# Group C's pooling behind group D's attention, with its two halves handled together

## The chip, the core and the metric

The kernel runs on one core of a Trainium2 chip. The metric is the device time of one execution in microseconds. Three runs of the kernel before gave 1563.94, 1564.75 and 1565.75 us; their median, 1564.75 us, is what a change is held against.

## The reference

Two layers of a transformer block over 512 latent and 256 context tokens, 1024 features each, all in 32-bit numbers. Each layer modulates and normalises its input, projects it, and gives the columns to four groups of 256 channels: A (windowed attention), B (gated position mixing), C (pooling), D (attention over a 2-D neighbourhood). Their outputs are joined, projected, gated and added; a feed-forward part follows. The last layer computes group C for the latent tokens alone. Group C is this:

```
for gi, w in enumerate((2, 4, 8, 16)):       # 64 channels each
    lo, hi = clip(t - w // 2, 0, n), clip(t - w // 2 + w, 0, n)
    pooled = (cs[:, hi] - cs[:, lo]) / (hi - lo) - y     # centred mean less the token
    outs.append(pooled @ w_pool[gi])
out_c = concatenate(outs) * scale
```

## The kernel before

Tokens lie along the free axis, 128 channels on the partitions. A layer begins with projections for group C (two tiles of 128 channels, c = 0 and 1) and for D's values, straight from the scaled input; c = 0 lands in the two pj banks of PSUM, c = 1 in the two sc banks, D's values in po, pt, tq and md. While they run, the normalised input h is made (L311 on POOL, L313 on DVE, L314 on ACT, L315 on DVE). L266 copies the shift out of PSUM.

Then come, in program order: the pooling of both c (c_pool), D's values, the query and key projections of D's first pair of heads (d_proj; in the last layer d_ctx before it makes the context keys of both pairs), the end of C (c_fin), the attention of pair 0 (d_group), the projections and the attention of pair 1, and then groups A and B. A projected tile goes through post_qk: ACT squares it (L479), DVE sums (L481), takes an inverse root in ten small steps (L100 to L109), multiplies (L484, which frees the pj or sc bank, and L486), PE transposes it into the one tq bank (L510), ACT and DVE write the query (L525, L526) and the key (L531 to L533) out of it. In the attention DVE takes the scores out of sc (L628, L630), ACT the exponential (L359), PE transposes (L337) and multiplies (L349), ACT copies the result to the mix tile (L354).

c_pool multiplies the PSUM tile by r (L788), ACT adds the shift (L789), POOL clears the margins (L784) and builds the sums over windows by repeated additions (L792 and L793 for c = 0, L795 to L798 for c = 1). Channels 0 to 63 end in one buffer and 64 to 127, with the wider window, in another, so DVE handles the halves one after the other: the edges (L806), then the scaling less the token (L807). L92 and L93 split the result into a high and a low part. c_fin multiplies by the pooling weights (wph) and ACT scales the result into the mix tile (L819).

What sets the order: the source fixes no order between engines. A planner simulates the whole program and gives each engine its queue; among instructions that are ready, the earlier one in the program goes first. On the chip each engine then works its queue in that order. Buffers have tags, each with so many buffers (BUFS and BANKS). Within a tag the planner gives them out in the order of the tiles' first writes in the program: a later tile gets none before the earlier ones have theirs. The st tag has 8 buffers. The eight scaled inputs fill it first; then come three tiles for each c (b1, b2, ph), then the keys and queries of D's pairs (the key's low half is cleared on POOL, L556, which needs nothing but the buffer), then those of A. The bias tag has 2; one of them holds wph until c_fin(1) is done, the others hold the bias tiles of the heads, which POOL builds (L612) from a table that SP loads (L606).

Of the kernel before, what the change touches and what calls it, by code (L numbers as in the profile page):

```python
# [8 lines left out]
F32 = mybir.dt.float32  # L9
F32R = mybir.dt.float32r  # L10
I32 = mybir.dt.int32
AF = mybir.ActivationFunctionType
OP = mybir.AluOpType
# [5 lines left out]
SEQ = 512  # L19
CTX = 256  # L20
NT = SEQ + CTX
# [7 lines left out]
BIG = 1e30  # L29
W = 24 + NT  # L30
BUFS = {"h": 8, "x": 8, "st": 8, "w": 6, "raw": 3, "mraw": 2, "T": 3, "pts": 3, "bias": 2, "row": 3, "post": 4,
        "br": 1}
BANKS = {"pj": 2, "sc": 2, "tq": 1, "pt": 1, "po": 1, "md": 1}
MAGIC = float(0x5F3759DF)
GELU_C = 0.7978845608028654
# [4 lines left out]
def hybrid_block(ctx: ExitStack, tc, t, out):  # L40
    nc = tc.nc
    V, S, G, T = nc.vector, nc.scalar, nc.gpsimd, nc.tensor
# [3 lines left out]
    small = ctx.enter_context(tc.tile_pool(name="small", bufs=4))  # L46
# [3 lines left out]
    def tile(tag, shape, dtype=F32):  # L50
        return sb.tile(shape, dtype, tag=tag, name=tag, bufs=BUFS[tag])
# [212 lines left out]
    def shift_of(cuts, pss):  # L264
        sh = small.tile([128, 2], F32, tag="sh", name="sh")
        V.tensor_copy(sh, pss[1][:, cuts[1]:cuts[1] + 2])  # L266
        return sh
# [117 lines left out]
    for l in range(DEPTH):  # L385
        last = l == DEPTH - 1
        segs = segs_lat if last else segs_all
# [11 lines left out]
        if l == 0:  # L399
# [3 lines left out]
            for what, k in START.split():  # L403
# [15 lines left out]
                if what + str(k) == "s5":  # L419
                    r = norm_spread(rr, segs_all, ("md", "md"))  # L420
            first = ws
            mods.append(new_mod(1))
        else:
            r = norm_spread(norm_scale(sq, segs_all), segs_all, ("tq", "tq"))
            first = [feat_units(*x) for x in first]
        fcuts = [cuts_lat if last else cuts_all] * 2 + [cuts_all]
        pss = [[psum(x) for x in y] for y in (("pj", "pj"), ("sc", "sc"), ("po", "pt"))]
# [13 lines left out]
        if l == 0:  # L441
# [3 lines left out]
            edge = const_tile("edge", [128, 2, 3, 8], t["edge"])  # L445
# [16 lines left out]
        V.memset(wpool, 0.0)  # L462
        for j in range(2):
            nc.sync.dma_start(wpool[64 * j:64 * j + 64, :, 64 * j:64 * j + 64], t["wpool"][l, j])
        wph = tile("bias", [128, 2, 256], F32R)
        split_to(wph[:, 0], wph[:, 1], wpool.rearrange("p a b -> p (a b)"))

        def lhs_nat(k, z, i):
# [100 lines left out]
        def d_proj(p, K=None):  # L569
            w = group_units("win_d", p)  # L570
            bs = (0, 2) if K else tiles
            K = K or d_keys()
            Q = tile("st", [128, 2, NT], F32R)
            for bi, b in enumerate(bs):
                ps = tok_proj(w, b, 0, 256, [["pj", "sc", "pj"], ["pj", "pj", "pj"]][p][bi])
                post_qk(ps, b, 2, 2, gd, 2, False, [Q], K, True)
            return Q, K
# [22 lines left out]
        mix = [None] * KT  # L600
# [176 lines left out]

        pos = {0: 8, 1: 16 + SEQ}

        def c_pool(c, pss):  # L780
            b1, b2 = tile("st", [128, 2, W]), tile("st", [128, 2, W])
            y, sA = b1[:, 0], b1[:, 1]
            sB, res = b2[:, 0], b2[:, 1]
            G.memset(y, 0.0)  # L784
            sh = shift_of(fcuts[0], pss)
            for (_, _, s0, s1, v, o), ps in zip(fcuts[0][0], pss):
                yv = y[:, pos[v] + s0 - SEQ * v:pos[v] + s1 - SEQ * v]
                V.tensor_mul(yv, ps[:, o:o + s1 - s0], r[:, s0:s1])  # L788
                S.activation(yv, yv, AF.Identity, bias=sh[:, v:v + 1])  # L789

            if c == 0:
                G.tensor_add(res[:, 1:W], y[:, 0:W - 1], y[:, 1:W])  # L792
                G.tensor_add(sA[64:128, 2:W - 1], res[64:128, 1:W - 2], res[64:128, 3:W])  # L793
            else:
                G.tensor_add(sA[:, 1:W], y[:, 0:W - 1], y[:, 1:W])  # L795
                G.tensor_add(sB[:, 2:W - 1], sA[:, 1:W - 2], sA[:, 3:W])
                G.tensor_add(res[:, 4:W - 3], sB[:, 2:W - 5], sB[:, 6:W - 1])
                G.tensor_add(sA[64:128, 8:W - 7], res[64:128, 4:W - 11], res[64:128, 12:W - 3])  # L798
            ph = tile("st", [128, 2, NT], F32R)
            for s0, s1, v in segs:  # L800
                n = s1 - s0
                o = pos[v]
                for q0, q1, src in ((0, 64, res), (64, 128, sA)):

                    for e, o1 in ((0, o), (1, o + n - 8)):
                        V.tensor_mul(src[q0:q1, o1:o1 + 8], src[q0:q1, o1:o1 + 8], edge[q0:q1, c, e])  # L806
                    V.scalar_tensor_tensor(sB[q0:q1, o:o + n], src[q0:q1, o:o + n], edge[q0:q1, c, 2, 0:1],  # L807
                                           y[q0:q1, o:o + n], op0=OP.mult, op1=OP.subtract)
                split_to(ph[:, 0, s0:s1], ph[:, 1, s0:s1], sB[:, o:o + n])
            return ph  # L810

        def c_fin(c, ph):
            mix[4 + c] = tile("x", [128, NT])
            for s0, s1, v in segs:
                n = s1 - s0
                ps = psum(["sc", "po", "sc", "tq"][2 * c + v])
                mm3(ps[:, :n], wph[:, 0, 128 * c:128 * c + 128], wph[:, 1, 128 * c:128 * c + 128],
                    ph[:, 0, s0:s1], ph[:, 1, s0:s1], True, True)
                S.activation(mix[4 + c][:, s0:s1], ps[:, :n], AF.Copy, scale=csc[:, c:c + 1])  # L819


        def d_group(p, Q, K, Vt):
            mix[6 + p] = tile("x", [128, NT])
            d_pair(p, Q, K, Vt)
            if not last:
                for i in (4, 5):
                    ctx_pair(i, Q, K[0], K[1],
                             [[Vt[:, x, 64 * hh:64 * hh + 64] for hh in range(2)] for x in (4, 5)], None, mix[6 + p])
# [9 lines left out]
                             nsink[:, p:p + 3:2], mix[p])  # L838

        if last:  # L840
            ph = [c_pool(c, pss[c]) for c in range(2)]
            v0 = d_values(pss[2], "row")
            v1 = d_values(pss[3], "mraw")
            kc = d_ctx()
            q0 = d_proj(0, kc[0])
            c_fin(0, ph[0])
            c_fin(1, ph[1])
            alt[:] = ["pt", "md"]
            d_group(0, *q0, v0)
            q1 = d_proj(1, kc[1])  # L850
            d_group(1, *q1, v1)
            ga = a_proj()
            a_group(0, *ga)
            gb = b_proj()
            a_group(1, *ga)
            b_fin(*gb)
        else:
            ph = [c_pool(c, pss[c]) for c in range(2)]
            v0 = d_values(pss[2], "row")
            v1 = d_values(pss[3], "mraw")  # L860
            q0 = d_proj(0)
            c_fin(0, ph[0])
            c_fin(1, ph[1])
            alt[:] = ["pt"]
            d_group(0, *q0, v0)
            q1 = d_proj(1)
            mod_unit(4, mods[l])
            mod_gain(mods[l], 1)
            d_group(1, *q1, v1)
            ga = a_proj()  # L870
            mod_unit(2, mods[l])
            a_group(0, *ga)
            gb = b_proj()
            b_fin(*gb)
            mod_unit(3, mods[l])
            alt[:] = ["pt", "md"]
            a_group(1, *ga)
# [26 lines left out]
        for mt in range(KT):  # L904
            w = wsplit(t["wout"][l, mt])
            outs = proj_out(w, KT, mh, ORDER, [[["pj", "pj", "tq", "md", "sc", "sc", "pt", "po"], ["pj", "pj", "tq", "md", "sc", "sc", "pt", "po"]][l][(mt * len(segs) + i) % 8] for i in range(len(segs))])
            x = xs[mt]
# [180 lines left out]
```

## Time and profile before

| | us |
|---|---|
| median of three runs | 1564.75 |
| the profiled execution | 1565.54 |
| its span, first to last instruction | 1563.8 |
| PE busy in it | 1518.4 |
| DVE busy | 963.7 |
| ACT busy | 618.1 |
| POOL busy | 122.2 |

How to read it: PE is the engine of matmuls, DVE, ACT and POOL work on vectors, SP issues DMAs. A matmul's end is modelled, and matmuls overlap, so a PE that is shown busy is not PE at its peak. Layer 0 has its projections for C and D up to some 80 us, then the attention up to some 310 us; in layer 1 the same stretches are 940 to 964 and 1035 to 1150 us. The rest is the output projection and the feed-forward part, where PE stands still hardly at all.

### The profile page before, as it was taken

To read this page: it belongs to the slowest core of one execution; us is meant where nothing else is said; L and a number is where in the kernel's file an instruction comes from. 1 tells how busy PE (TensorE), PEld (TensorE's weight loads), DVE (VectorE), ACT (ScalarE), POOL (GpSimd) and SP (SyncE) were. 2 spreads that over 40 slices of the span, in tenths; PEclk is the share of its full clock that TensorE was granted. 3 is DMA by queue.
4 is the path that set the end of the run, shared out by engine and by line. 5 is a ranking of instruction groups with operands and counts; after the bars stand their busy time and mean duration, and the time that the engine had idled before them with its cause. 6 is when DMAs were issued, how large, how long until landed. Compare 5 with 4: busy or idle time off the path is not lost.

```text
span 1563.8 us, 26196 instructions
## 1 busy us (share of the span) xinstructions
PE 1518.4 (97%) x10098; PEld 1336.1 (85%) x10098; DVE 963.7 (62%) x2335; ACT 618.1 (40%) x1276; POOL 122.2 (8%) x107
## 2 busy tenths in 40 slices
PE   7889999999999999999999998899999999999999
PEld 4668888788888888888888887788889998998997
DVE  4797876686485624833384467789856543454453
ACT  5546655643322112221222354457654332332331
POOL 2431000000000000000000005632000000000000
PEclk9899999999999999999999999999999999999999
DMA  8433133342243313622272231111223333223323
GB/s 309 122 115 116 48 110 129 122 139 75 88 142 113 117 62 115 222 59 64 93 248 59 78 113 55 58 55 47 81 82 102 95 84 105 90 87 102 95 82 100
DMA packets 79325, 163.39 MB, mean 104 GB/s; under 512 B 12001, under 2 KB 17761, under 8 KB 79201
## 3 DMA queue, kind: packets, MB, share of 16 engines
q1 hardware_dynamic: 79200, 161.73, 32.8%
q8 instruction: 79, 1.29, 0.3%
q14 instruction: 46, 0.37, 0.1%
HBM read 157.50 MB, written 4.19 MB: 103 GB/s over the span
## 4 chain that ended last, share of the span: by engine, by line
PE 89%; DVE 5%; ACT 1%; issue 0%; DVEq 0%; ACTq 0%
PE pj L65 9%; PE pj L66 9%; PE pj L67 9%; PE sc L66 6%; PE sc L65 6%; PE sc L67 6%; PE tq L65 3%; PE po L349 3%; PE tq L66 3%; PE tq L67 3%; PE po L65 3%; PE po L66 3%; PE po L67 3%; PE pt L66 2%; PE pt L67 2%; PE pt L65 2%
## 5 line engine op out<-in xcount | busy, mean ns | idle before, releaser
L82 ACT ACTIVATE w<-raw 128x512 fp32r<-128x512 f32 x368 | 227.5, 621 | 640.1 <-PE sc L67 159.5
L83 DVE TENSOR_TENSOR w<-raw,w 128x512 fp32r<-128x512 f32 x336 | 227.3, 679 | 244.7 <-ACT w L82 244.2
L65 PE MATMUL pj<-w,h 128*128 128x256 f32 x480 | 141.5, 295 | 12.8 <-DVE post L484 6.7
L66 PE MATMUL pj<-w,h 128*128 128x256 f32 x480 | 140.0, 292 | 2.9 <-DVE w L83 2.9
L67 PE MATMUL pj<-w,h 128*128 128x256 f32 x480 | 139.4, 291 | 0.0
L65 PE MATMUL pj<-st,w 128*128 128x258 f32 (+2 forms) x384 | 120.6, 314 | 2.5 <-ACT st L253 2.3
L66 PE MATMUL pj<-st,w 128*128 128x258 f32 (+2 forms) x384 | 120.4, 314 | 0.7 <-DVE st L254 0.7
L66 PE MATMUL sc<-st,w 128*128 128x258 f32 (+2 forms) x384 | 120.0, 313 | 0.0
L65 PE MATMUL sc<-st,w 128*128 128x258 f32 (+2 forms) x384 | 119.9, 312 | 0.0
L67 PE MATMUL pj<-st,w 128*128 128x258 f32 (+2 forms) x384 | 119.8, 313 | 0.0
L67 PE MATMUL sc<-st,w 128*128 128x258 f32 (+2 forms) x384 | 119.2, 311 | 0.0
L65 PEld LDWEIGHTS pj<-w,h 128*128 128x128 f32 x480 | 94.4, 197 | 21.1 <-issue 9.3
L83 POOL TENSOR_TENSOR w<-raw,w 128x512 fp32r<-128x512 f32 x32 | 44.2, 1398 | 742.2 <-ACT w L82 721.7
L66 PEld LDWEIGHTS pj<-w,h 128*128 128x128 f32 x480 | 94.7, 197 | 4.4 <-DVE w L83 3.1
L67 PEld LDWEIGHTS pj<-w,h 128*128 128x128 f32 x480 | 94.3, 197 | 1.3 <-issue 1.2
L65 PEld LDWEIGHTS pj<-st,w 128*128 128x128 f32 x384 | 73.1, 191 | 9.5 <-ACT st L253 3.5
L66 PEld LDWEIGHTS pj<-st,w 128*128 128x128 f32 x384 | 72.8, 190 | 5.7 <-DVE st L254 0.9
L67 PEld LDWEIGHTS pj<-st,w 128*128 128x128 f32 x384 | 72.7, 190 | 5.7 <-issue 1.7
L65 PEld LDWEIGHTS sc<-st,w 128*128 128x128 f32 x384 | 73.2, 191 | 4.6
L66 PEld LDWEIGHTS sc<-st,w 128*128 128x128 f32 x384 | 72.8, 189 | 4.4
L67 PEld LDWEIGHTS sc<-st,w 128*128 128x128 f32 x384 | 72.4, 189 | 4.2
L65 PE MATMUL po<-st,w 128*128 128x512 f32 (+1 forms) x192 | 66.5, 346 | 0.0
(304 smaller groups left out, 4125.8 us busy)
## 6 DMA issues: line engine op xcount, KB each, us to landing
mraw<-in_wmod SPq DMA_DIRECT2D x80, 512.0 KB, 3.7
raw<-in_wg SPq DMA_DIRECT2D x88, 256.0 KB, 2.6
raw<-in_wu SPq DMA_DIRECT2D x88, 256.0 KB, 2.6
raw<-in_wd SPq DMA_DIRECT2D x64, 256.0 KB, 2.7
h<-in_wslab SPq DMA_DIRECT2D x16, 512.0 KB, 7.8
raw<-in_wout SPq DMA_DIRECT2D x32, 256.0 KB, 2.6
x<-in_xt SPq DMA_DIRECT2D x16, 384.0 KB, 5.8
raw<-in_wd SPq DMA_DIRECT2D x32, 192.0 KB, 2.4
```

Source lines behind the costliest of these rows:

```text
L65: T.matmul(ps, ah, bh, start=start, stop=False)
L66: T.matmul(ps, ah, bl, start=False, stop=False)
L67: T.matmul(ps, al, bh, start=False, stop=stop)
L82: S.activation(w[:, 0, :n], raw, AF.Copy)
L83: eng.tensor_sub(w[:, 1, :n], raw, w[:, 0, :n].bitcast(F32))
L349: T.matmul(o[64 * hh:64 * hh + 64, :128], vs[hh][lo:hi], pts[i, hh], start=i == 0, stop=i == n - 1)
```

## The change

c_pool is parted. c_take stays where c_pool was: it takes a tile of c out of PSUM with the multiplication by r, into the mix tile of c itself, and copies the shift to a small buffer of its own. The rest of c_pool moves: c_pool(0) and c_fin(0) stand behind the attention of D's pair 0, c_pool(1) and c_fin(1) behind that of pair 1. In it, ACT brings the shift in on the way from the mix tile to the padded row y; the rows end at n, which is 792 elements in layer 0 as before and 528 in the last layer; ACT copies channels 64 to 127 of the sums into the buffer of the others, and the edges, the scaling and the subtraction then run once on 128 partitions. wph gets a buffer with a tag of its own.

```diff
-        wph = tile("bias", [128, 2, 256], F32R)
+        wph = tile("wph", [128, 2, 256], F32R)
...
-        def c_pool(c, pss):
+        def c_take(c, pss):
+
+            mix[4 + c] = tile("x", [128, NT])
+            for (_, _, s0, s1, v, o), ps in zip(fcuts[0][0], pss):
+                V.tensor_mul(mix[4 + c][:, s0:s1], ps[:, o:o + s1 - s0], r[:, s0:s1])
+            sh = small.tile([128, 2], F32, tag="csh", name="csh", bufs=2)
+            V.tensor_copy(sh, pss[1][:, fcuts[0][1]:fcuts[0][1] + 2])
+            return sh
+
+        def c_pool(c, sh):
             b1, b2 = tile("st", [128, 2, W]), tile("st", [128, 2, W])
             y, sA = b1[:, 0], b1[:, 1]
             sB, res = b2[:, 0], b2[:, 1]
-            G.memset(y, 0.0)
-            sh = shift_of(fcuts[0], pss)
-            for (_, _, s0, s1, v, o), ps in zip(fcuts[0][0], pss):
-                yv = y[:, pos[v] + s0 - SEQ * v:pos[v] + s1 - SEQ * v]
-                V.tensor_mul(yv, ps[:, o:o + s1 - s0], r[:, s0:s1])
-                S.activation(yv, yv, AF.Identity, bias=sh[:, v:v + 1])
+            n = pos[segs[-1][2]] + segs[-1][1] - segs[-1][0] + 8
+            up = slice(64, 128)
+            G.memset(y[:, :n], 0.0)
+            for s0, s1, v in segs:
+                S.activation(y[:, pos[v]:pos[v] + s1 - s0], mix[4 + c][:, s0:s1], AF.Identity, bias=sh[:, v:v + 1])
...
-                G.tensor_add(sA[64:128, 2:W - 1], res[64:128, 1:W - 2], res[64:128, 3:W])
+                G.tensor_add(sA[up, 2:n - 1], res[up, 1:n - 2], res[up, 3:n])
+                S.activation(res[up, 2:n - 1], sA[up, 2:n - 1], AF.Copy)
...
-                G.tensor_add(sA[64:128, 8:W - 7], res[64:128, 4:W - 11], res[64:128, 12:W - 3])
+                G.tensor_add(sA[up, 8:n - 7], res[up, 4:n - 11], res[up, 12:n - 3])
+                S.activation(res[up, 8:n - 7], sA[up, 8:n - 7], AF.Copy)
...
-                for q0, q1, src in ((0, 64, res), (64, 128, sA)):
-
-                    for e, o1 in ((0, o), (1, o + n - 8)):
-                        V.tensor_mul(src[q0:q1, o1:o1 + 8], src[q0:q1, o1:o1 + 8], edge[q0:q1, c, e])
-                    V.scalar_tensor_tensor(sB[q0:q1, o:o + n], src[q0:q1, o:o + n], edge[q0:q1, c, 2, 0:1],
-                                           y[q0:q1, o:o + n], op0=OP.mult, op1=OP.subtract)
+
+                for e, o1 in ((0, o), (1, o + n - 8)):
+                    V.tensor_mul(res[:, o1:o1 + 8], res[:, o1:o1 + 8], edge[:, c, e])
+                V.scalar_tensor_tensor(sB[:, o:o + n], res[:, o:o + n], edge[:, c, 2, 0:1],
+                                       y[:, o:o + n], op0=OP.mult, op1=OP.subtract)
...
-            mix[4 + c] = tile("x", [128, NT])
...
-            ph = [c_pool(c, pss[c]) for c in range(2)]
+            csh = [c_take(c, pss[c]) for c in range(2)]
...
-            c_fin(0, ph[0])
-            c_fin(1, ph[1])
             alt[:] = ["pt"]
             d_group(0, *q0, v0)
+            c_fin(0, c_pool(0, csh[0]))
             q1 = d_proj(1)
...
             d_group(1, *q1, v1)
+            c_fin(1, c_pool(1, csh[1]))
             ga = a_proj()
```

The calls at the end are those of layer 0; in the last layer c_fin and c_pool move in the same way.

## Rows read from the trace of the kernel before

**Rows 1.** Of the profile's page: busy time, share and instructions of each engine
```profile
PE 1518.4 (97%) x10098; PEld 1336.1 (85%) x10098; DVE 963.7 (62%) x2335; ACT 618.1 (40%) x1276; POOL 122.2 (8%) x107
```

**Rows 2.** Stretches, as from:to and length, then each engine's busy time, clock, DMA
```profile
80.00:90.00 10.00, 8.01 (x54) 8.02 (x55) 9.31 (x25) 3.74 (x8) 1.47 (x2) 0.83 0.26 79
...
110.00:120.00 10.00, 8.02 (x46) 5.12 (x47) 8.93 (x33) 4.21 (x11) 0.00 (x0) 0.83 0.59 208
126.00:166.00 40.00, 40.00 (x335) 35.44 (x334) 32.25 (x129) 27.97 (x72) 7.84 (x11) 1.00 0.32 106
...
970.00:980.00 10.00, 7.11 (x47) 7.14 (x48) 8.23 (x21) 3.98 (x9) 3.00 (x2) 0.68 0.00 0
...
1000.00:1010.00 10.00, 6.45 (x41) 6.43 (x41) 9.04 (x31) 2.03 (x5) 3.57 (x5) 0.83 0.19 56
...
1035.00:1080.00 45.00, 45.00 (x388) 40.38 (x387) 43.00 (x165) 35.06 (x93) 15.33 (x14) 1.00 0.17 50
```

**Rows 3.** PE's waits from 76 to 122 us: total, times, longest
```profile
PE tq L510 <- DVE st L533: 3.2, 1, 3.2
PE pj L66 <- DVE w L83: 2.9, 1, 2.9
```

**Rows 4.** PE's waits from 958 to 1032 us
```profile
PE pj L65 <- DVE post L484: 6.7, 3, 3.5
PE pj L65 <- DVE st L788: 6.1, 1, 6.1
PE tq L510 <- DVE st L533: 3.5, 1, 3.5
```

**Rows 5.** DVE's groups by shape, 60 to 125, then 965 to 1010 us
```profile
L806 DVE TENSOR_TENSOR st<-st,edge 64x8 f32<-64x8 f32 x16 | 3.7, 292 | 0.1
...
L807 DVE SCALAR_TENSOR_TENSOR st<-st,edge 64x512 f32<-64x512 f32 x4 | 3.0, 747 | 0.1
...
L807 DVE SCALAR_TENSOR_TENSOR st<-st,edge 64x256 f32<-64x256 f32 x4 | 1.9, 478 | 0.0
...
L93 DVE TENSOR_TENSOR st<-st 128x512 fp32r<-128x512 f32 x2 | 1.4, 682 | 0.0
...
L806 DVE TENSOR_TENSOR st<-st,edge 64x8 f32<-64x8 f32 x8 | 3.4, 460 | 0.5 <-POOL st L792 0.4
...
L807 DVE SCALAR_TENSOR_TENSOR st<-st,edge 64x512 f32<-64x512 f32 x4 | 3.0, 748 | 0.2
```

**Rows 6.** DVE in order of time: start, length, line, operation, shape, count
```profile
77.35 3.65 DVE L315 SCALAR_TENSOR_TENSOR h<-x,mod,h 128x512 fp32r<-128x512 f32 x2
...
91.03 0.17 DVE L104 SCALAR_TENSOR_TENSOR ry<-rz,ry 128x8 f32<-128x8 f32 x1
91.22 1.38 DVE L105 TENSOR_TENSOR rz<-ry 128x8 f32<-128x8 f32 x1
...
95.89 0.69 DVE L484 TENSOR_TENSOR post<-pj,ry 128x512 f32<-128x512 f32 x1
96.61 1.37 DVE L486 TENSOR_TENSOR post<-post,d_q_gain 128x256 f32<-128x256 f32 x1
```

**Rows 7.** POOL in order of time, 60 to 130 us
```profile
91.07 1.50 POOL L795 TENSOR_TENSOR st<-st 128x791 f32<-128x791 f32 x1 [9.54 <-DVE rz L103]
...
95.85 1.85 POOL L798 TENSOR_TENSOR st<-st 64x777 f32<-64x777 f32 x1
...
103.54 3.10 POOL L556 MEMSET st<- 64x768 f32 x4
128.87 1.23 POOL L612 TENSOR_TENSOR bias<-dmask,br 128x256 f32<-128x256 f32 x1 [22.24 <-PE sc L368]
```

**Rows 8.** ACT in order of time, around 1006 and 1060 us
```profile
1005.72 0.63 ACT L92 ACTIVATE st<-st 128x512 fp32r<-128x512 f32 x1 [6.54 <-DVE st L807]
...
1057.14 0.28 ACT L354 ACTIVATE x<-po 128x128 f32<-128x128 f32 x1
...
1062.21 0.36 ACT L531 ACTIVATE st<-tq 64x256 fp32r<-64x256 f32 x1
```

More of the change, by code (lines that the diff above doesn't have):

```diff
@@ L31 @@
 BUFS = {"h": 8, "x": 8, "st": 8, "w": 6, "raw": 3, "mraw": 2, "T": 3, "pts": 3, "bias": 2, "row": 3, "post": 4,
-        "br": 1}
+        "br": 1, "wph": 1}
 BANKS = {"pj": 2, "sc": 2, "tq": 1, "pt": 1, "po": 1, "md": 1}
@@ L783, in c_pool @@
             sB, res = b2[:, 0], b2[:, 1]
-            G.memset(y, 0.0)
-            sh = shift_of(fcuts[0], pss)
-            for (_, _, s0, s1, v, o), ps in zip(fcuts[0][0], pss):
-                yv = y[:, pos[v] + s0 - SEQ * v:pos[v] + s1 - SEQ * v]
-                V.tensor_mul(yv, ps[:, o:o + s1 - s0], r[:, s0:s1])
-                S.activation(yv, yv, AF.Identity, bias=sh[:, v:v + 1])
+            n = pos[segs[-1][2]] + segs[-1][1] - segs[-1][0] + 8
[3 more added lines that the diff above has]
+                S.activation(y[:, pos[v]:pos[v] + s1 - s0], mix[4 + c][:, s0:s1], AF.Identity, bias=sh[:, v:v + 1])
             if c == 0:
-                G.tensor_add(res[:, 1:W], y[:, 0:W - 1], y[:, 1:W])
-                G.tensor_add(sA[64:128, 2:W - 1], res[64:128, 1:W - 2], res[64:128, 3:W])
-            else:
-                G.tensor_add(sA[:, 1:W], y[:, 0:W - 1], y[:, 1:W])
-                G.tensor_add(sB[:, 2:W - 1], sA[:, 1:W - 2], sA[:, 3:W])
-                G.tensor_add(res[:, 4:W - 3], sB[:, 2:W - 5], sB[:, 6:W - 1])
-                G.tensor_add(sA[64:128, 8:W - 7], res[64:128, 4:W - 11], res[64:128, 12:W - 3])
+                G.tensor_add(res[:, 1:n], y[:, 0:n - 1], y[:, 1:n])
+                G.tensor_add(sA[up, 2:n - 1], res[up, 1:n - 2], res[up, 3:n])
+                S.activation(res[up, 2:n - 1], sA[up, 2:n - 1], AF.Copy)
+            else:
+                G.tensor_add(sA[:, 1:n], y[:, 0:n - 1], y[:, 1:n])
+                G.tensor_add(sB[:, 2:n - 1], sA[:, 1:n - 2], sA[:, 3:n])
+                G.tensor_add(res[:, 4:n - 3], sB[:, 2:n - 5], sB[:, 6:n - 1])
+                G.tensor_add(sA[up, 8:n - 7], res[up, 4:n - 11], res[up, 12:n - 3])
+                S.activation(res[up, 8:n - 7], sA[up, 8:n - 7], AF.Copy)
             ph = tile("st", [128, 2, NT], F32R)
@@ L857, in hybrid_block @@
         else:
-            ph = [c_pool(c, pss[c]) for c in range(2)]
+            csh = [c_take(c, pss[c]) for c in range(2)]
             v0 = d_values(pss[2], "row")
@@ L861, in hybrid_block @@
             q0 = d_proj(0)
-            c_fin(0, ph[0])
-            c_fin(1, ph[1])
             alt[:] = ["pt"]
             d_group(0, *q0, v0)
+            c_fin(0, c_pool(0, csh[0]))
             q1 = d_proj(1)
@@ L869, in hybrid_block @@
             d_group(1, *q1, v1)
+            c_fin(1, c_pool(1, csh[1]))
             ga = a_proj()
```

## The prediction

> **What bounds the kernel now.** I read the engines' busy times first: PE is busy 97% of the span, so 45 us is all that it ever stands still [rows 1], and only a change that shortens PE's stops can pay. The stretches of ten us come next: they show where those stops lie. Apart from the start (out of reach of this change), they stand in two places, behind the first projections of each layer, where group C's pooling is done: 76 to 122 us in layer 0 and 958 to 1032 us in layer 1. There DVE is busy 8.2 to 9.3 us of ten while PE is not full, and the granted clock, once PE has stood still for 3 us and more, falls to 0.83 or 0.68 of 2.4 GHz over the slice: for a part of it, it is at its lower level of 1.2 [rows 2 to 4]. Third, PE's own waits in the two windows: in layer 0 it waits 3.2 us for L533 (DVE's last step of a query/key tile, which frees the tq bank) and 2.9 us for L83 (a weight split on DVE) [rows 3]; in layer 1, 6.7 us for L484, 6.1 us for L788 (pooling's own eviction of its PSUM bank) and 3.5 us for L533 [rows 4]. All of them are on DVE. In the attention behind it PE shows full: 40.00 of 40 and 45.00 of 45 us, with DVE at 32.25 of 40 in layer 0, but at 43.00 of 45 in layer 1 [rows 2]. So the question is what DVE is spared before the attention, and what it can't take inside it.
>
> **The change, part by part.**
> *Halves together.* L806 and L807 run once on 128 partitions instead of twice on 64. An instruction's time here goes by its elements per partition, so half of the instructions go: in layer 0 half of 3.7 + 3.0 + 1.9 us = 4.3 us, in layer 1 half of 3.4 + 3.0 = 3.2 us [rows 5]. For it ACT copies the upper half: four copies, of 789 (layer 0) and 525 elements. The nearest row is ACT's split of 512 elements at 0.63 us [rows 8]; by size 0.97 and 0.65 us, 3.2 us in all. ACT has 28 of 40 and 35 of 45 us busy there [rows 2], so I take zero, and 3.2 if they end on a chain that PE waits for.
> *Shorter rows in layer 1.* With n = 528 instead of 792, POOL's steps there shrink by a third.
> *c_take.* The multiplications by r stay, at the same place in the order, but write into an x buffer (free once the first h is made), so the second one no longer waits for c = 0 to be pooled. About 0.68 + 0.41 us of DVE (the size of the split row [rows 5] and its smaller form) comes forward in layer 0. PE's 6.1 us for L788 I leave: the multiplication still stands behind all of L313 and L315.
> *wph in its own buffer.* Today the second bias tile of pair 0 waits until c_fin(1) has given its buffer back: POOL stands 22.24 us in front of L612 in layer 0 [rows 7]. It can now run before the window. Only queued POOL work gains; nothing on PE's path, zero, and at most one L612 (1.23 us) either way.
> *Pooling moved.* Two orders hold it back. It stands behind d_group in the program, and the planner hands out st buffers in program order: POOL's clearing of the key tiles, which needs only a buffer, stands behind the whole pooling, at 103.54 us [rows 7]. The same rule now puts the pooling behind the key and query tiles of pair 0, so it can't creep forward into idle engines. It issues no DMA. c_fin's 12 and 6 matmuls move with it at the same PE time; their sc bank now comes between the scores of pair 0 and pair 1, where the second sc bank covers it: zero, up to 1.4 us a call.
>
> What leaves the early window in layer 0: three kinds of cost. DVE's own steps are the 8.6 us named above and 2.2 us of splits. POOL's six additions (1.50 to 1.85 us each, 9.7 us in all) hold DVE up: L105, a step on 8 elements, takes 1.38 us beside L795, where the like step L104 ahead of it takes 0.17 [rows 6, 7]; there are three of that kind, and with the 0.95 us of L486 and the 2.3 us lost in the pair of L315 at 77.35 us (3.65 us, where two steps of their size would take some 1.4) this is 6.9 us, 0.7 us of DVE for each us of POOL. And ACT, in order, stands 6.54 us in front of a split of the pooling in layer 1 while the key tile's L531, which frees tq, is queued behind it [rows 8].
>
> An instruction with one operand in PSUM didn't wait: L484 took 0.69 us beside L798, and L486 behind it, all in SBUF, 1.37 us [rows 6, 7]. The Trainium skill, in "SBUF — State Buffer", section "Who interferes with whom", says the same as a rule: a DVE instruction with two SBUF inputs contends with GpSimd's reads, one with at most one does not; by it, much of the attention's DVE work (L628, L630 and L533 read PSUM) would be untouched by the moved additions, and the lock terms below would be about half.
>
> *Layer 0, gained.* The 3.2 us behind L533 go with the queue ahead of it. Of the 2.9 us behind L83, the L315 pair gives back 2.3 and c_take's second multiplication takes 1.1: 1.2 us gone. Two slices at 0.83 are 3.4 us each at half speed, 1.7 us lost each [rows 2]; I count one. 3.2 + 1.2 + 1.7 = 6.1 us, between 3 and 9.5 (all of both stalls and both slices).
> *Layer 0, given back.* The attention gets 4.3 + 2.2 us of DVE steps and 0.7 x 9.7 = 6.8 us of waiting, 13.3 us. DVE has 7.75 us idle in 126 to 166 us [rows 2], and half of the load (c = 1) falls later still: between 0 and 5.5 us, nearest to 0; I take 1.5.
> *Layer 1, gained.* Behind L484 and L533 lie 10.2 us. What stands in the way there are 8.3 us of pooling on DVE, ACT's 6.54 us, and POOL's pooling; the weight splits on POOL stay and hold DVE up as before. I take two thirds, 6.8 us, and one of two slices at 0.83, 1.7: 8.5 us, between 3 and 13.6.
> *Layer 1, given back.* 3.2 us of steps, 1.4 of splits, 0.7 x 6.5 = 4.5 us of waiting: 9.1 us, where DVE has 2.0 us idle in 45 [rows 2]. Between 0 and 7.1; c = 0 has to be over before pair 1's query tile gets its buffer, so half lies earlier. 3.5, and 1.25 for group A's key tile, which now waits for the last st buffer of c = 1 (between 0 and rival B): 4.75 us.
> Sum: -6.1 + 1.5 - 8.5 + 4.75 = -8.35 us. The profiled execution took 1565.54 us (span 1563.8), 0.8 us over the median of 1564.75: 1557.2 on its scale, **1556.5 us** on the median's.
>
> **The rivals.**
> *A, the cost only moves.* DVE is the limit inside the attention too, and the page's full PE hides it: matmul times overlap, and PEld shows 40.38 of 45 us [rows 2]. Then all that is moved comes back: 5.5 + 7.1 + 1.25 and ACT's 3.2 on the chain, 17 against 14.6 gained: +2.4, about 1567 us. For it: 43.00 of 45 us in layer 1. Against: layer 0's idle DVE, and that 7.5 us are really gone. The Trainium skill, "Trainium Kernel Development and Optimization", section "Performance Expectations", calls matmul busy time a bad metric and LDWEIGHTS busy a good one, which would make this rival likelier.
> *B, slower: group A starves behind the pooling of c = 1.* Its last st buffers need pair 0's tiles back, and group A's key tile comes after them. Today the first key write (L531 at 1062.21) follows pair 0's last output (L354 at 1057.14) by 5.1 us [rows 8]. Afterwards three additions, a copy, the edges, one L807 and a split stand between: in layer 1 3.3 + 0.65 + 0.6 + 0.75 + 0.63 = 5.9 us, in layer 0 4.9 + 0.97 + 1.2 + 1.2 + 0.63 = 8.9 us. Behind a DVE that is 96% busy I put twice that: 11.8 and 17.8, later than today by 6.7 and 12.7. If PE has nothing else then, 19.4 us are lost, and with 3.5 + 1.5 of the give-back against 14.6 gained: +9.8, 1575 us. It decides from some 10 us between the last output of pair 0 and the first key write. Against it: PE has the modulation's matmuls in layer 0, and pj is projected one tile ahead.
> *C, the pooling stays early* because idle engines draw it forward; only the halving counts, 7.5 us of DVE, half on the path: 1561 us. Against it: the order of the buffers.
> *D, nothing is given back* and all stalls but L788's go: 9.5 + 13.6 = 23.1 us, 1542 us.
>
> **How the numbers follow.** Forecast 0.51 (own range 1549 to 1561.5), A 0.20, B 0.15, C 0.06, D 0.08. From 1545 to 1569 all but D and most of B is held, some 0.8. About 3.1 us, 0.2%, is what a measurement here can tell from no change. Faster: the forecast, D, half of C: 0.62. Same: most of A, the rest of C: 0.21. Slower: B and a little of A: 0.17.
>
> **What would show it.** Right: no POOL addition between the first projections and the first scores of either layer; L104 to L109 at some 0.17 us in layer 0; PE's waits for L533 gone from both windows, L788's 6 us still there; slices at 1.00 around 110 and 1000 us. Wrong on the give-back: PE idle, or fewer matmuls per ten us, between the pairs' attentions, with DVE at 100%. B: more than 10 us from pair 0's last L354 to group A's first L531, with PE idle in it. C: additions still beside L105.

## The result, and the profile after

The changed kernel takes 1556.64 us (median of 4 runs, 1555.05 to 1557.38) against 1564.36 us of the kernel before on the same chip: 7.7 us less by the medians. The ratio on record is 0.9945, 95% interval 0.9933 to 0.9957, which is 8.6 us of 1564.75 (6.7 to 10.5); the text goes by these ratios. The forecast was 1556.5. The number came out; half of its sum did not, as the experiments show.

The page of the changed kernel, profiled at 1556.92 us (span 1555.1), busy time of each engine:

```profile
PE 1514.8 (97%) x10098; PEld 1332.3 (86%) x10098; DVE 957.6 (62%) x2317; ACT 620.8 (40%) x1278; POOL 113.6 (7%) x107
```

PE has as many matmuls as before and is busy 3.6 us less [rows 1]: PE's own time has changed too, not only its stops.

The stretches, with the columns of [rows 2]:

```profile
80.00:90.00 10.00, 10.00 (x81) 9.03 (x80) 6.18 (x17) 3.87 (x7) 0.00 (x0) 1.00 0.40 133
110.00:120.00 10.00, 10.00 (x76) 7.89 (x74) 9.27 (x32) 5.51 (x12) 0.76 (x1) 1.00 0.31 105
...
970.00:980.00 10.00, 10.00 (x80) 10.00 (x80) 3.86 (x13) 4.92 (x9) 4.65 (x4) 0.93 0.21 64
1000.00:1010.00 10.00, 5.13 (x31) 4.95 (x31) 9.47 (x21) 5.92 (x12) 7.09 (x6) 0.78 0.24 79
1035.00:1080.00 45.00, 42.67 (x353) 36.56 (x352) 42.28 (x146) 32.59 (x85) 16.96 (x17) 1.00 0.18 58
```

PE's waits from 76 to 122 us, then from 950 to 1032 us (total, times, longest):

```profile
PE pj L65 <- DVE post L484: 0.6, 1, 0.6
PE pj L65 <- DVE x L784: 0.5, 1, 0.5
```

```profile
PE pj L65 <- DVE x L784: 7.2, 1, 7.2
PE pj L65 <- ACT st L532: 4.9, 1, 4.9
PE tq L510 <- DVE st L533: 0.6, 1, 0.6
```

The window of layer 0 is clear: the 6.1 us of [rows 3] are 1.1, and both slices that stood at 0.83 [rows 2] are at 1.00, with 81 and 76 matmuls for 54 and 46. In layer 1 the multiplication that empties C's bank (now L784) holds PE as long as L788 did [rows 4]; of the 10.2 us behind L484 and L533, 5.5 are left. The 4.9 us put down to L532 end on L484, which runs at 1005.80 us. In the attention of layer 1 PE has 353 matmuls in 45 us where it had 388, partly since it comes to them earlier.

How far PE has come by 120 and by 220 us, before and then after (the count behind PE's busy time is its matmuls):

```profile
0.00:120.00 120.00, 96.78 (x635) 74.09 (x636) 84.54 (x210) 61.05 (x122) 42.53 (x34) 0.93 0.54 182
...
0.00:220.00 220.00, 196.78 (x1451) 158.62 (x1452) 166.57 (x517) 125.04 (x288) 53.35 (x47) 0.96 0.43 143
```

```profile
0.00:120.00 120.00, 101.58 (x698) 79.40 (x698) 79.86 (x203) 60.85 (x121) 33.04 (x33) 0.94 0.54 188
...
0.00:220.00 220.00, 200.10 (x1484) 161.28 (x1484) 162.02 (x497) 124.34 (x286) 48.44 (x47) 0.97 0.43 146
```

At 120 us the changed kernel leads by 63 matmuls, some 8 us at 81 in ten us; at 220 us by 33.

The same instructions in both traces (us, start in the profiled execution):

| | before | after | difference |
|---|---|---|---|
| layer 0: first score of group D (L628) | 127.2 | 128.0 | +0.8 |
| its last | 200.0 | 194.5 | -5.5 |
| first of group A (L708) | 215.4 | 225.1 | +9.7 |
| its last | 301.4 | 298.5 | -2.9 |
| first FFN norm (L290) | 378.1 | 375.3 | -2.8 |
| end of the FFN of layer 0 (L290) | 941.9 | 936.5 | -5.3 |
| layer 1: first score of group D (L628) | 1036.0 | 1021.4 | -14.6 |
| its last | 1079.8 | 1072.9 | -6.9 |
| last of group A | 1143.8 | 1136.5 | -7.3 |
| FFN norm of layer 1 | 1189.4 | 1182.1 | -7.3 |
| end | 1560.8 | 1552.1 | -8.6 |

Of 8.6 us, 2.8 lie in the mixing of layer 0, 2.0 in that of layer 1, and 2.5 and 1.4 in the two FFNs, where the change touches nothing and PE stands full in both kernels. A first score can come later with PE further on: at D's first score in layer 0 PE has 763 matmuls behind it instead of 694, because projections that follow the score in the old order now run ahead of it.

### The profile page after: what moved, and what is told of

The parts are those of the page before. It is cut to its first block, busy times and chain, and to the rows that moved or that the text cites. A ratio compares the mean times of both kernels' runs of the same rounds, so it can differ in the third digit from the quotient of the medians.

```text
span 1555.1 us, 26167 instructions
## 1 busy us (share of the span) xinstructions
PE 1514.8 (97%) x10098; PEld 1332.3 (86%) x10098; DVE 957.6 (62%) x2317; ACT 620.8 (40%) x1278; POOL 113.6 (7%) x107
## 4 chain that ended last, share of the span: by engine, by line
PE 88%; DVE 6%; DMA 3%; ACT 1%; issue 1%; SPq 0%; POOL 0%; ACTq 0%; POOLq 0%
PE pj L65 9%; PE pj L66 9%; PE pj L67 9%; PE sc L65 6%; PE sc L66 6%; PE sc L67 6%; PE tq L65 3%; PE tq L66 3%; PE po L66 3%; PE po L65 3%; PE tq L67 3%; PE po L67 3%; PE po L349 3%; PE pt L66 2%; PE pt L65 2%; PE pt L67 2%
## 5 line engine op out<-in xcount | busy, mean ns | idle before, releaser
L83 DVE TENSOR_TENSOR w<-raw,w 128x512 fp32r<-128x512 f32 x336 | 226.2, 676 | 241.2 <-ACT w L82 240.5
L65 PE MATMUL pj<-st,w 128*128 128x258 f32 (+2 forms) x384 | 120.2, 314 | 1.4 <-ACT st L253 1.2
L65 PEld LDWEIGHTS pj<-w,h 128*128 128x128 f32 x480 | 93.3, 194 | 20.4 <-issue 10.4
L83 POOL TENSOR_TENSOR w<-raw,w 128x512 fp32r<-128x512 f32 x32 | 42.6, 1342 | 747.5 <-ACT w L82 723.0
L66 PEld LDWEIGHTS pj<-w,h 128*128 128x128 f32 x480 | 93.4, 195 | 1.8 <-issue 0.9
L67 PEld LDWEIGHTS pj<-w,h 128*128 128x128 f32 x480 | 93.2, 194 | 0.4 <-issue 0.3
```

Source lines behind the costliest of these rows:

```text
L65: T.matmul(ps, ah, bh, start=start, stop=False)
L66: T.matmul(ps, ah, bl, start=False, stop=False)
L67: T.matmul(ps, al, bh, start=False, stop=stop)
L83: eng.tensor_sub(w[:, 1, :n], raw, w[:, 0, :n].bitcast(F32))
```

## The experiments

Each run was compared with the kernel before on the same chip. The table has them all: the ratio with its interval, what it is in us of 1564.75, what of that lies in the FFNs' matmuls, and the rest. The FFN part is worked out from the starts of successive matmuls with a scaled x tile (st) in the trace: in layer 0 the mean step is 233.94 ns before and 232.38 after at 512 columns, 120.37 and 119.48 at 258; times 1056 of each that is 1.65 + 0.94 = 2.6 us; in layer 1, worked out alike, 1.4 us. Single executions of one kernel lie up to 5 us apart, so the verdicts go by the ratio and the traces only tell where. "The rest" is the ratio's microseconds less the FFN part; its uncertainty is that of the ratio, 1.4 to 2.6 us either way.

| kernel | median us | ratio (95%) | us | of it FFN | rest |
|---|---|---|---|---|---|
| changed kernel | 1556.64 | 0.9945 (0.9933 to 0.9957) | -8.6 | -4.0 | -4.6 |
| e1 wph's own buffer alone | 1569.77 | 1.0028 (1.0019 to 1.0037) | +4.4 | 0 | +4.4 |
| e2 all but the move | 1565.38 | 0.9998 (0.9989 to 1.0007) | -0.3 | -0.6 | +0.3 |
| e3 moved, halves apart | 1555.15 | 0.9931 (0.9918 to 0.9943) | -10.8 | -4.0 | -6.8 |
| e4 only c = 1 moved | 1559.70 | 0.9964 (0.9952 to 0.9977) | -5.6 | -3.4 | -2.2 |
| e5 only c = 0 moved | 1561.44 | 0.9976 (0.9967 to 0.9986) | -3.8 | -1.9 | -1.9 |
| e6 c = 1 behind A's projections | 1560.35 | 0.9971 (0.9962 to 0.9980) | -4.5 | -3.2 | -1.3 |
| e7 no additions, no copies | 1549.61 | 0.9900 (0.9886 to 0.9913) | -15.6 | -4.6 | -11.1 |
| f1 before, other places in the FFN | 1561.77 | 0.9975 (0.9966 to 0.9984) | -3.9 | -4.0 | +0.1 |
| i1 e3, c_take earlier | 1554.78 | 0.9931 (0.9918 to 0.9943) | -10.8 | -4.0 | -6.8 |
| i2 e3, c = 0 behind pair 1's projections | 1556.63 | 0.9941 (0.9928 to 0.9955) | -9.2 | -3.8 | -5.4 |
| i3 e3, c_take into post in layer 1 | 1551.11 | 0.9909 (0.9893 to 0.9926) | -14.2 | -4.0 | -10.2 |
| i4 i3 with halves together | 1556.26 | 0.9945 (0.9931 to 0.9958) | -8.6 | -4.0 | -4.6 |

My theory going in was the forecast's: the pooling's DVE steps and POOL's additions cost PE's early stops, and moving them frees these, less what the attention gives back. The first rival came from the table of starts: half of the gain is made in the FFNs.

**e1, wph alone.**

```diff
-        wph = tile("bias", [128, 2, 256], F32R)
+        wph = tile("wph", [128, 2, 256], F32R)
```

> Only one edit: the kernel before, with wph in a buffer of its own. The forecast prices the wait that this takes away at nothing, within one L612 (1.2 us): 1563.2 to 1564.6 us. Rival (placement): about 3.9 us of the 7.7 us gained by the change lie in the two FFN stretches, where PE stands full in both kernels and the 512-column matmuls merely follow each other after 233.2 instead of 234.2 ns. If the new tile alone shifts what sits where and brings this, the run takes 1560 to 1562 us and shows the 233.2 ns; if it stays at 234.2 ns, the new tile is not the cause.

It is 4.4 us slower, by more than either theory allowed. The places in the FFN are those of the kernel before and so are the steps (233.94 and, in layer 1, 120.18 ns), so the tile itself is not what speeds the FFN up. The 3.5 us lost in layer 0 stand between group D's last score (+0.4) and A's last (+3.5); in between the planner has put PE's matmuls in another order. One thing that the new order does can be seen: POOL builds the first bias tile (L612) at 59.74 us, ahead of the L311 steps that make h, and not at 128.87 us as before [rows 7]. Which part of the order costs the 4.4 us I could not show.

**e2, all but the move.**

```diff
             csh = [c_take(c, pss[c]) for c in range(2)]
+            ph = [c_pool(c, csh[c]) for c in range(2)]
...
             q0 = d_proj(0)
+            c_fin(0, ph[0])
+            c_fin(1, ph[1])
             d_group(0, *q0, v0)
-            c_fin(0, c_pool(0, csh[0]))
```

> The changed kernel with the pooling put back to its old place (behind the first evictions, ahead of pair 0's values), all else of the change kept: halves together, shorter rows, copy of the upper half by ACT, wph's own buffer. If the move is what pays (forecast), the waits behind L533 and L484 come back and only half of the 7.5 us of DVE that the merging spares counts: about 1560.5 us, 1559 to 1563. If the merging alone pays, it stays at 1556 to 1558. If the merging pays nothing and ACT's copies stand on the path: 1564 to 1567, no better than before.

No gain at all. L105 takes 1.73 us again beside the additions, and PE waits 3.5 us for L533 in layer 0, as in [rows 3]. Against e1, all that e2 adds (the halves together, the shorter rows and c_take) is worth 4.7 us here, where DVE is short (0.6 of it in the FFNs); it just pays for wph. What each of the three brings was not tried. Against the changed kernel the move is worth 8.3 us, 3.4 of it in the FFNs.

**f1, the places in the FFN.** The kernel before, with the eight buffers of the scaled x tiles claimed first and dealt out by a list:

```diff
+        given = [tile("st", [128, 2, NT + 2], F32R) for _ in range(KT)]
+        for x in given:
+            G.memset(x[:, 0, 0:8].bitcast(F32), 0.0)
...
-            h.append(scaled(x, a[:, 1, mt], sh[:, 0:1].to_broadcast([128, 2]) if last else sh, segs))
+            h.append(scaled(x, a[:, 1, mt], sh[:, 0:1].to_broadcast([128, 2]) if last else sh, segs,
+                            given[[[3, 2, 0, 4, 7, 6, 1, 5], [7, 0, 3, 1, 2, 4, 6, 5]][l][mt]]))
```

> The kernel before, its attention and pooling untouched; only the eight st buffers that hold the scaled x tiles through each FFN are dealt out in another order, the one that they have in the changed kernel (layer 0: places 2,0,6,5,1,4,7,3 instead of 6,7,0,2,5,3,4,1; layer 1: 6,2,7,5,3,0,1,4 instead of 6,2,1,4,3,0,5,7). Seen so far: kernels with the same order show the same mean step between 512-column matmuls in the FFN of layer 0 (233.94 ns before and with wph alone, 234.03 with the pooling early; 232.38 changed, 232.37 with the halves apart). If the order of places makes this difference: the step falls to 232.4 ns, 120.18 ns in layer 1 to 119.5, and the time by 2.6 + 1.4 = 4.0 us, to 1560.4 us, with every stop of PE in 76 to 122 us as before. If the step hangs on what DVE, ACT and the DMAs do meanwhile: 233.9 ns and 1564.4 us.

Measured 232.45 and 119.52 ns, and 3.9 us less (2.5 to 5.3): as this theory has it. A stretch inside the FFN of layer 0, f1 and then e1, which has the order of the kernel before:

```profile
400.00:900.00 500.00, 500.00 (x2864) 433.54 (x2863) 273.42 (x524) 126.89 (x223) 0.00 (x0) 1.00 0.37 114
```

```profile
400.00:900.00 500.00, 500.00 (x2849) 432.12 (x2848) 269.77 (x518) 125.83 (x220) 0.00 (x0) 1.00 0.36 113
```

PE is full in both, and does 15 matmuls more in f1. In the early window f1 waits as before (3.3 us for L533). The changed kernel has 2864 there too. So 4.0 of its 8.6 us come from the order in which its moved pooling hands back st buffers.

**e3, halves apart at the new place.**

```diff
-                S.activation(res[up, 2:n - 1], sA[up, 2:n - 1], AF.Copy)
...
-                S.activation(res[up, 8:n - 7], sA[up, 8:n - 7], AF.Copy)
...
-                    V.tensor_mul(res[:, o1:o1 + 8], res[:, o1:o1 + 8], edge[:, c, e])
...
+                for q0, q1, src in ((0, 64, res), (64, 128, sA)):
...
+                        V.tensor_mul(src[q0:q1, o1:o1 + 8], src[q0:q1, o1:o1 + 8], edge[q0:q1, c, e])
```

> The changed kernel in its new order, but the last steps of the pooling done for each half of the partitions by itself as before (no copy on ACT; edges and L816 twice on 64 partitions). DVE has some 4.3 us more in layer 0 and 3.2 us more in layer 1 minus what shorter rows spare, all inside the attention; ACT has four copies less. If DVE is the limit in the attention of layer 1 (96% busy before) the 2 to 3 us there come on top and little in layer 0: 1558 to 1560.5. If PE hides it: 1556.3 to 1557.3. If ACT's copies were on the path: faster, 1554 to 1556.

Faster, if anything: 2.2 us, with intervals that overlap. The last run (i4) settles the sign. The profiled execution of e3 took 1550.96 us, the fastest of its five, so its trace makes the difference look larger than it is.

**e4 and e5, one c at a time.** Only where c_pool and c_fin of the other c are called differs.

> The changed kernel, but the pooling of c = 0 at its old, early place; only c = 1 is moved. By the forecast c = 1 holds four of the six additions and all that stand beside L105, so most of what the move gains (8 us between the merged pooling early and the changed kernel) comes with it: 1557 to 1559.5 us, with less given back in layer 1's attention, where c = 0's pooling no longer stands in front of pair 1. If the gain needs the whole window free: 1561 to 1564. If c = 0 is what costs in the attention: 1554 to 1556.

> The changed kernel, but the pooling of c = 1 at its old, early place; only c = 0 is moved. By the forecast little of the gain is left: 1561 to 1564 us, with L105 again over 1 us. Group A's first key write in layer 0, at 181.5 us in the changed kernel and some 14 us earlier before, should come back to 165 to 170 us, since no buffer of c = 1 stands ahead of it; if that delay cost PE time, this kernel gains it back and comes out at 1556 to 1559 all the same.

Outside the FFNs c = 1 alone brings 2.2 us, c = 0 alone 1.9 us against 4.6 for both: about equal parts, though c = 1 has four of the six additions. In e5 L531 of group A comes without a gap again (group A's first key of layer 0 is written at 167.3 us), and the kernel is the slower one all the same; but c = 1's early pooling costs it time as well, so this alone doesn't price the key tile.

**e6, group A's tiles first.**

```diff
-            c_fin(1, c_pool(1, csh[1]))
             ga = a_proj()
+            c_fin(1, c_pool(1, csh[1]))
```

> The changed kernel with the pooling of c = 1 put one step further back, behind the projections of group A, so that group A's key and query tiles get st buffers before the pooling does. The forecast's term for group A's key tile waiting for the pooling's last buffer is 1.25 us: 1555.4 us if it is right, with the first key write (L531) no longer behind L816. If the queue in front of it costs nothing: 1556.3 to 1557. If pooling now collides with group A's attention instead, or its PSUM bank comes late: 1558 to 1561.

Slower than the changed kernel by 4.1 us, 0.8 of it in the FFNs. There is a gap to close: in the changed kernel nothing is written to a key tile of layer 0 for 22 us, the stretch in which c = 1 has its last additions and its split. ACT in order of time, and the stretch behind (columns as in [rows 2]):

```profile
159.52 0.38 ACT L531 ACTIVATE st<-tq 64x256 fp32r<-64x256 f32 x1
181.51 0.36 ACT L531 ACTIVATE st<-tq 64x256 fp32r<-64x256 f32 x1
```

```profile
180.00:200.00 20.00, 19.27 (x137) 12.76 (x137) 15.88 (x58) 15.07 (x39) 2.58 (x2) 1.00 0.56 188
```

The same stretch before:

```profile
180.00:200.00 20.00, 20.00 (x157) 15.56 (x155) 17.56 (x57) 13.25 (x33) 2.98 (x2) 1.00 0.21 61
```

Before, group A's first key was written at 167.66 us. In e6 it is written at 162.19 us, and A's first score still comes at 225.6 us (225.1 changed): an early key tile alone doesn't bring it forward. e6 can't show more, since c = 1's last three additions now run from 209.72 to 214.71 us, right ahead of that score. e3 and i3 can: there A's first key is as late (179.4 and 181.3 us), and PE keeps its lead over the kernel before past it. Matmuls that PE has behind it, one execution each:

| by | before | changed | e3 apart | i3 apart | i4 together |
|---|---|---|---|---|---|
| 120 us | 635 | 698 | 705 | 692 | 711 |
| 160 us | 963 | 1026 | 1036 | 1023 | 1041 |
| 220 us | 1451 | 1484 | 1525 | 1509 | 1476 |
| 300 us | 2082 | 2097 | 2145 | 2125 | 2091 |

From 160 to 220 us the changed kernel loses 30 matmuls of its lead and i4 loses 53; e3 and i3, with the same additions some 159 to 166 us into the run as in the other two, lose at most 2. The traced executions of i3 and i4 lie within 1.1 us of their medians. So what layer 0 gives back there goes with the halves being handled together, and not with the late key tile or the additions alone.

**e7, no additions.**

```diff
-                G.tensor_add(res[:, 1:n], y[:, 0:n - 1], y[:, 1:n])
...
-                S.activation(res[up, 8:n - 7], sA[up, 8:n - 7], AF.Copy)
...
-                    V.tensor_mul(res[:, o1:o1 + 8], res[:, o1:o1 + 8], edge[:, c, e])
+                    V.tensor_mul(y[:, o1:o1 + 8], y[:, o1:o1 + 8], edge[:, c, e])
```

> The changed kernel without the pooling's additions on POOL and without ACT's copies of the upper half: the last steps read the cleared and filled row itself, so that c = 0 and c = 1 get no sums. DVE's own steps stay. This prices what the additions still cost at their new place. By the forecast they hold DVE up by 0.7 us for each of theirs, 6.8 us in layer 0 (mostly hidden) and 4.5 us in layer 1 (mostly given back): 1551 to 1554 us. If DVE loses nothing to POOL there, or PE has other work: 1555.5 to 1557. With the halves apart, without the copies, it was 1554: a result near that says that it is the copies and not the additions.

7.0 us less than the changed kernel, 6.5 outside the FFNs: additions and copies together still cost that at their new place. Against e3, which has the additions and no copies, it is 4.3 us outside the FFNs, with e3's doubled last steps on DVE in it. Their price on DVE can be read beside them. DVE in the changed kernel, while L805 to L807 run on POOL (161.34 to 166.42 us):

```profile
160.64 0.43 DVE L533 TENSOR_TENSOR st<-tq,st 64x256 fp32r<-64x256 f32 x1
161.10 1.95 DVE L495 TENSOR_TENSOR post<-post,sinT 128x64 f32<-128x64 f32 x4
163.09 0.42 DVE L651 TENSOR_REDUCE mn<-sc 128x1 f32<-128x256 f32 x1
163.43 1.27 DVE L497 TENSOR_TENSOR post<-post,cosT 128x256 f32<-128x256 f32 x1
164.62 0.41 DVE L651 TENSOR_REDUCE mn<-sc 128x1 f32<-128x256 f32 x1
164.95 1.75 DVE L498 TENSOR_TENSOR post<-post 128x256 f32<-128x256 f32 x1
```

L498 takes 0.42 us alone. L651, which reads sc in PSUM, takes the same beside an addition as without, and so do L533 (0.43 us at 106.45 us beside L801) and L484 (0.42 at 1047.99 beside L807), with one operand in PSUM. One operand in SBUF is no safeguard by itself: L362, a TENSOR_SCALAR on 448 elements, takes 1.25 us at 1043.85 us beside L806, 0.45 alone. Summed over the instructions that overlap an addition, DVE loses 13.5 us to 19.1 us of additions before (0.71 each) and 8.4 to 16.3 us after (0.52 over all twelve, four of which stand ahead of the first scores). Two of the steps are left out: L497, since it has no like alone, and L101 at 1001.20 us, which stands beside a weight split nearly all of its time.

**i2, c = 0 one step later** (from e3: c_fin(0, c_pool(0, ...)) behind d_proj of pair 1).

> The kernel with the halves apart (1555.2 us), and the pooling of c = 0 one step further back, behind the projections of pair 1, so that pair 1's query tile gets its st buffer first and POOL's two additions move out of the stretch ahead of the first scores (L800 at 1002.4 us in layer 1 stood beside the rsqrt steps in front of PE's 4.9 us wait). If the additions there are what that wait is made of, it falls to 3 us or less: 1551 to 1553.5 us beside the FFN's part. If the wait hangs on POOL's weight splits (L83), it stays at 4 to 5 us: 1554.5 to 1556. As with c = 1 behind group A's projections (+4 us), moving it past the projections may cost more than it brings: 1557 to 1560. The order of the x tiles' places changes too, so the FFN's steps are compared apart.

The wait stays, and so it does with no additions at all. PE's waits in layer 1, i2 and then e7:

```profile
PE pj L65 <- DVE post L484: 5.0, 1, 5.0
```

```profile
PE pj L65 <- DVE post L484: 5.3, 1, 5.3
```

**i1 and i3, c_take ahead of the h tiles in layer 1.** In i1 the call alone moves (behind the tiles k = 1 and 2); in i3 it stands one tile earlier and also writes into post:

```diff
+            if last and k in (0, 1):
+                csh.append(c_take(len(csh), pss[len(csh)]))
...
-            mix[4 + c] = tile("x", [128, NT])
+            took[c] = tile("post", [128, 512]) if last else tile("x", [128, NT])
```

> The kernel with the halves apart (1555.2 us), and in layer 1 alone the multiplications by r that empty group C's two PSUM banks stand behind the second and third h tile on DVE instead of behind all eight. In the changed kernel PE waits 7.2 us there for them (at 968.6 us), as it did 6.1 us before. If that wait comes from the queue of h steps ahead of them on DVE, as the prediction says, it falls to 2 to 4 us, and the whole to 1550.5 to 1553.5 us; the places of the x tiles in the FFN are the same, so nothing comes from there. If PE then merely waits for the later h tiles, which are now about 1 us later each, or for L484: 1554.5 to 1556.5 us.

> Once more the kernel with the halves apart (1555.2 us). Writing the multiplications earlier in the program had left them at the same place on DVE, behind all of L313 and L315, because their x buffers come free only there; the wait was 7.2 us as before. Here they write into post buffers in layer 1, and stand on DVE between the L313 steps. If PE's 7.2 us hang on the queue ahead of them, the wait falls to 2 to 4 us and the time to 1550.5 to 1553.5 us. If the h tiles are late by themselves, the same stop shows behind L315 instead and the time stays at 1554 to 1556.5. Two of four post buffers are held until the pooling: if the steps of L484, which write there, stall for it, 1557 to 1561.

In i1 DVE's order stayed as it was, the multiplication still behind L315, and nothing moved: an experiment that did not do what it was meant to. In i3 it did. PE's waits in layer 1, i1 (L442 is the multiplication) and then i3 (L547 is L533 of the changed kernel, L498 its L484):

```profile
PE pj L65 <- DVE x L442: 7.2, 1, 7.2
```

```profile
PE tq L524 <- DVE st L547: 7.3, 1, 7.3
PE pj L67 <- DVE h L315: 2.9, 1, 2.9
PE pj L65 <- DVE post L498: 1.7, 1, 1.7
PE pj L65 <- DVE csh L444: 0.7, 1, 0.7
```

The 7.2 us go, and nearly as much comes up 35 us later behind L533. The time falls by 3.4 us against e3 all the same, though the intervals overlap, to 1551.11 us, the fastest version here that computes the pooling: its interval lies below that of the changed kernel. The traces put 2.4 us of that into layer 1's mixing.

**i4, i3 with the halves together.**

> The changed kernel with halves together, and with the multiplications of layer 1 in post buffers as in the kernel that took 1551.1 us; against that one only the handling of the halves differs (ACT's four copies, half of the last DVE steps). A second look at what the merging is worth at the pooling's new place: halves apart was 1.5 us the faster, within the uncertainty. If ACT's copies cost there, as the first pair hints: 1552 to 1554 us. If the DVE steps spared count: 1547 to 1550 us. If neither can be told: 1550.3 to 1551.9, and the four copies and the spared DVE steps are even.

5.6 us slower than i3, with intervals apart and the same places in the FFN. Together with e3 that is two pairs of the same sign: at its new place the merging costs 2 to 6 us. The traces have the loss in layer 0 (end of its FFN at 938.0 for 932.9 us in i3, 936.5 for 930.8 in the other pair). It is not simply the chain through ACT's copy: in i4 the copy starts 5.5 us after the addition it waits for, yet the split of c = 1 behind it starts at 172.73 us in i4 and at 172.75 in i3. Where PE loses it can be read, i3 and then i4:

```profile
176.00:205.00 29.00, 29.00 (x234) 23.54 (x231) 24.30 (x87) 18.59 (x49) 2.58 (x2) 1.00 0.50 166
```

```profile
176.00:205.00 29.00, 27.87 (x207) 20.16 (x205) 20.18 (x75) 18.52 (x50) 2.58 (x2) 1.00 0.44 148
```

Ahead of it the queue of loads differs: SP issues four loads of modulation weights from 162.69 to 177.25 us in i3, and nothing from 158.9 to 182.9 us in i4 (160.4 to 182.4 in the changed kernel), where a load of weights stands in front that waits for L83 on POOL. Whether that is the cause was not tried, so what exactly costs it stays open.

## Why the prediction was right, and where it wasn't

**The total** was right by a chance of two errors. The sum of -8.35 us holds no term for the FFN, which brought 4.0. The steps that it does hold brought 4.6: too much by 3.7 us.

**Layer 0, gained: right in place.** The waits for L533 and L83 went, and the slices came to 1.00. L104 to L109 take 0.17 us in the rsqrt chains at 90 and 101 us; of two that are longer up to 110 us one stands beside a weight split on POOL. Of the other, L100 and L101 stand beside the end of L801 and POOL's clearing of a key tile. In size the term was too small, if anything: the first score did not come forward (+0.8), but at 120 us PE leads by 63 matmuls, an estimated 8 us at 81 in ten us, against the 6.1 us of the sum.
**Layer 0, given back: too small.** 1.5 us were allowed, and the net gain is 2.8 instead of 4.6. Against the estimated 8 us some 5 came back, over three times the term. And it came by another way than the one priced: the prediction put it on DVE's load, moved steps and moved additions alike, but e3 and i3 carry that load too and keep the lead up to 220 us. In these traces it goes with the halves handled together, whose copies were taken at zero.
**Layer 1.** The wait for L788 stayed, as the prediction said, and for the reason it gave: i1 and i3 show that it hangs on the place behind L313 and L315. Of L484's and L533's 10.2 us, 4.7 went, not 6.8; the slice at 1000 us is at 0.78, and not 1.00. By D's first score the gain is an estimated 6.5 us of the 8.5 (14.6 less the 5.3 brought along, less some 2.7 for the 23 matmuls that PE is then short of, at 388 in 45 us); 4.5 of it came back, near the 4.75 charged. (The 8.3 us of pooling on DVE that the prediction names there are 7.8 by its own terms, 3.4 + 3.0 + 1.4.) Net 2.0 us against 3.75. The prediction's remark that the weight splits on POOL stay and hold DVE up is what is left: the 5 us wait for L484 stands without any addition (e7, i2), and L100 and L101 in front of it take 1.17 and 1.23 us beside L83.
**The place of the additions: wrong.** I wrote that no addition would stand between the first projections and the first scores. POOL in order of time:

```profile
104.63 1.51 POOL L800 TENSOR_TENSOR st<-st 128x791 f32<-128x791 f32 x1 [3.19 <-ACT st L797]
106.22 1.56 POOL L801 TENSOR_TENSOR st<-st 64x789 f32<-64x789 f32 x1
```

```profile
1002.36 1.06 POOL L800 TENSOR_TENSOR st<-st 128x527 f32<-128x527 f32 x1
...
1006.58 1.06 POOL L801 TENSOR_TENSOR st<-st 64x525 f32<-64x525 f32 x1
```

The first scores are at 128.0 and 1021.4 us. The order of buffers puts c = 0 behind pair 0's key and query tiles; I took that for behind its scores, and these tiles are written well before.
**The lock of 0.7 us for each us of POOL** holds for the early window (0.71) and is too high for the new places (0.52), where L533, L628, L651 and L484 stand beside additions and read PSUM. The Trainium skill, "SBUF — State Buffer", section "Who interferes with whom", says that a DVE instruction with at most one input in SBUF doesn't contend with GpSimd, except in its 2-port modes, which it says TENSOR_SCALAR can enter. L533 and L651 agree with the first, L362 looks like the second. I left the exception out, so my "about half" by the rule (0.35) came out as much too low as 0.7 was too high.
**ACT's copies and the halves**: taken at zero, at most 3.2 us. Early, the merging pays, with shorter rows and c_take (4.7 us together, e1 to e2). Late it costs 2.2 and 5.6 us in the two pairs, once under and once over the bound. The step that failed is to carry a saving of DVE's time over to a place where, by e3 and i4, it brings nothing.
**wph**: taken at zero, at most 1.2 us. Alone it costs 4.4. What failed is the assumption that a freed buffer only moves the work that waited for it: in e1 PE's matmuls come in another order as well.
**Group A's key tile**: 1.25 us were charged. Its delay is there and larger (13.9 us in layer 0), yet e6, which takes it away, is slower, and e3 and i3 have it without PE losing ground. For rival B I also misread the rows: L354 at 1057.14 is pair 0's second output and not its last [rows 8], so its basis of 5.1 us is void.
**The rivals.** A (all comes back): refuted, since the move keeps 4.9 us outside the FFNs between e2 and the changed kernel. B's delay took place without its price: PE waits 1.4 us in all between D's first score in layer 0 and A's. C: part of the pooling did stay early, but not beside L105. D: refuted, 1556.6 us is far from 1542, and e7 shows that additions and copies still cost 6.5 us outside the FFNs.

## What to carry to other kernels

When a change reorders buffers of one tag, look whether a later stage that PE fills changes its pace: compare matmul counts of equal stretches there before crediting the time to the stage that was edited. Where an edit lets work change places, compare how many matmuls are done by a time, and not when one marked instruction starts. Price each edit of a bundle by a run of its own, since here wph's buffer, the rework of the pooling and the move are worth +4.4, -4.7 and -8.3 us, and a part that pays where an engine is short can cost where it isn't. To move an instruction in a planned order, see what holds it first: here it was the buffer it writes, not its line in the program.

## What the runs showed of the hardware

The step between two 512-column matmuls at full clock (1.00) depends on which buffers of the same tag the moving tiles lie in: 233.94 ns before and 232.38 ns after as a mean, and 232.45 ns in f1, where in the FFN only these places differ from before. By position within a chain of eight tiles it goes from some 230 to 237 ns before and from 230 to 234 after. The pattern by position repeats within 0.4 ns between kernels with the same order of places (before and e2), and f1 took over that of the changed kernel within 0.3 ns. In layer 1, at 256 and 258 columns, the means lay between 119.0 ns (e7) and 120.2. What in a place makes the difference was not tried.
